# Other orders of reading the moving columns in the series of products behind the last store

## The chip, the core and the metric

The kernel runs on one core of one Trainium2 chip. Its time is the device time of one execution in microseconds (us); the times shown are medians of several executions. A profile is one further execution, recorded instruction by instruction. Its span runs from the first recorded instruction to the last.

## The reference, cut to what matters

The kernel computes one layer of an encoder: two token mixers side by side (windowed attention and a mixture of dilated attentions), merged by gates, then a dense channel mixer, each followed by a layer norm.

```
proj  = h @ w_in
o_a   = windowed_gqa_sink(qa, ka, va, a_sink)
o_b   = dilated_mixture(qb, kb, vb)
gates = sigmoid(h @ w_gate + b_gate)
mixed = g_a * (o_a @ w_br_a) + g_b * (o_b @ w_br_b)
h     = layer_norm(DN_ALPHA * h + mixed @ w_out)
f     = (silu(h @ w_ff_gate) * (h @ w_ff_up)) @ w_ff_down
out   = layer_norm(DN_ALPHA * h + f)
```

There are 512 tokens, 1024 features and 2816 hidden features in the channel mixer. The series of products that the change touches is no part of this: it works on copies of a finished piece of the output, and nothing reads what it leaves in PSUM.

## The kernel before

All work is entered as operations with the engines that may do them, a priority and the tiles that they read and write; a planner in the class Program (lines 100 to 260) places them by estimated costs and emits the instructions in that order. Operations of equal rank keep the order in which they were entered. The tiles are slots of 128 partitions x 512 columns of fp32 (2 KB on each partition, `slot`), wider tiles of 128 x 4 x 512 (`x4`), and eight PSUM banks of 128 x 512 (`bank`).

A product is `mm(out, weights, moving)`: the 128 x 128 weights are loaded into TensorE (LDWEIGHTS, engine PEld in the profile), and then the moving columns, up to 512, are streamed through (MATMUL, engine PE). Most products of the layer read operands of type fp32r, in runs of 256 or 512 columns that follow each other in memory: lines 452 to 454, 1110 to 1112, 1323 to 1325 and 1533 to 1535. Line 932 is one product of the layer that reads its columns, and writes its output, in runs of 32 that do not follow each other.

The last product of the layer is at line 1112, and the last store is issued by SP at line 1569. Behind it lines 1577 to 1616 add a series that the layer doesn't need:

- Lines 1578 to 1586: ACT copies the finished piece xt[3, 1] seven times, into w, x, y (fp32r), u, v (fp32) and b, c (bf16).
- Line 1590: `W(i)` is one of the four 128 x 128 blocks of w; A and B are two PSUM banks.
- `sections` (lines 1594 to 1614) is one operation on PE. Each line of it is a section: 16 products of one kind (8 for fp32, where each product is two instructions), one behind the other, in the order of the text.
- Lines 1595 to 1599 read x in sequence, 512 columns, with varying banks and weights. Lines 1600 to 1604 do the same with 256 columns. Line 1605 uses 64 rows, 1606 and 1607 bf16, 1608 and 1609 fp32. Line 1610 takes its weights with a step of four columns. Line 1611 reads x as two halves in turn: column 0, column 256, column 1, column 257, and so on. Line 1612 has 128 columns, 1613 an output of 64 rows, and 1614 is a series of transposes.

Sections read data that do not change while they run, so no section waits for another engine once the copies are there; the first product waits for the copies into w and x.

Of the kernel before, what the change touches and what calls it, by code (L numbers as in the profile page):

```python
# [15 lines left out]
P = 128  # L16
# [29 lines left out]
PE, ACT, DVE, POOL, SP = "PE", "ACT", "DVE", "POOL", "SP"  # L46
# [53 lines left out]
class Program:  # L100
# [15 lines left out]
    def op(self, alts, fn, reads=(), writes=(), prio=0.0, after=(), abs_prio=None, moves=0.0, extra=0):  # L116
        o = Op()
        o.alts, o.fn = alts, fn
        o.prio = (self.T + prio if abs_prio is None else abs_prio, len(self.ops))
        o.ready, o.done, o.eng = 0.0, None, None  # L120
        deps = set(a for a in after if a is not None)
        for t in reads:
            deps.update(self.writer.get(t, ()))
        for t in writes:
            deps.update(self.writer.get(t, ()))
            deps.update(self.readers.get(t, ()))
        deps.discard(o)
        for t in reads:
            self.readers.setdefault(t, []).append(o)
        for t in writes:  # L130
            self.writer[t] = [o]
            self.readers[t] = []
        o.bufs, o.new = [], []
        o.strict, o.moves, o.extra = self.strict, moves, extra
        o.hold = self.hold and prio <= -150
        for t in list(reads) + list(writes):
            b = self.buf_of(t)
            if b not in o.bufs:
                o.bufs.append(b)
                b.users += 1  # L140
        o.succ = []
        o.left = len(deps)
        for d in deps:
            d.succ.append(o)
        self.ops.append(o)
        return o
# [134 lines left out]
def hybrid_layer(ctx: ExitStack, tc: tile.TileContext, wpack, xT, xtok, sink, bgate,  # L281
                 ln1g, ln1b, ln2g, ln2b, ropec, ropes, maska, maskb, identd, out):
    nc = tc.nc
# [9 lines left out]
    op = pr.op  # L293
    mm = nc.tensor.matmul
    cnt = [0]

    def name(s):
        cnt[0] += 1
        return f"{s}{cnt[0]}"

    def slot(dt=F32, cls=None):
        cls = cls or "gen"
        return Buf("slot", cls, lambda: slab.tile([P, S], dt, tag="slab", bufs=N_SLOT, name=name("sl")))

    def bank(cls):
        return Buf("bank", cls, lambda: psum.tile([P, S], F32, tag="bank", bufs=8, name=name("ps")))

    def x4():
        return Buf("x4", None, lambda: slab.tile([P, 4, S], F32R, tag="x4", bufs=4, name=name("x4")))
# [4 lines left out]
    def fixed(shape, nm):  # L314
        b = Buf("fixed", None, None)
        b.tile = slab.tile(shape, F32, tag=nm, bufs=1, name=nm)
        return b


    def copy(eng, dst, src):  # L320
        if eng == ACT:
            nc.scalar.activation(dst, src, AF.Copy)  # L322
        else:
            nc.vector.tensor_copy(dst, src)
# [61 lines left out]
    ident = fixed([P, P], "ident")  # L386
# [29 lines left out]
    for j in range(KD):  # L416
        st, ap = slot(F32, "xs"), FIRST["x"][j]

        for c0, c1 in ((0, S // 2), (S // 2, S)) if j == 0 else ((0, S),):
            w, sk = c1 - c0, (st, c0)  # L420
# [5 lines left out]
               reads=[sk], writes=[th], abs_prio=ap)  # L426
            op([(DVE, dve(w))], lambda e, j=j, st=st, c0=c0, c1=c1: nc.vector.tensor_tensor(  # L427
                xl[j]()[:, c0:c1], st.t[:, c0:c1], f32(xh[j]()[:, c0:c1]), op=ALU.subtract), reads=[sk, th],
               writes=[tl], abs_prio=ap)
# [8 lines left out]
       reads=[nsink], writes=[nsink], abs_prio=-119)  # L438
# [607 lines left out]
    for f in range(16):  # L1046
        op([(ACT, act(S))], lambda e, f=f: nc.scalar.activation(gz[f].t, gz[f].t, AF.Sigmoid),
           reads=[gz[f]], writes=[gz[f]], after=exps)
# [11 lines left out]
    for f in range(8):  # L1060
        ps = bank("dense")
        wu = unit(U_BRA + f)
        for k in range(KD):
            feat_k(ps, wu, k, MA, lambda k: list(sa[k]))
        mark = op([(DVE, dve(S))], lambda e, f=f, ps=ps: nc.vector.tensor_tensor(gz[f].t, gz[f].t, ps.t, op=ALU.mult),
                  reads=[gz[f], ps], writes=[gz[f]], prio=EV)
# [4 lines left out]
    for f in range(8):  # L1071
# [3 lines left out]
        for k in range(2):  # L1075
            feat_k(ps, wu, k, MB, lambda k: list(sb_[k]), nk=2, col=lambda k, f=f: (k, (f % 4) * P))
        op([(DVE, dve(S))], lambda e, f=f, ps=ps: nc.vector.tensor_tensor(gz[8 + f].t, gz[8 + f].t, ps.t, op=ALU.mult),
           reads=[gz[8 + f], ps], writes=[gz[8 + f]], prio=EV)
        op([(DVE, dve(S))], lambda e, f=f: nc.vector.tensor_tensor(gz[f].t, gz[f].t, gz[8 + f].t, op=ALU.add),
           reads=[gz[f], gz[8 + f]], writes=[gz[f]], prio=EV)  # L1080
# [3 lines left out]
    xt = {(t, j): slot() for t in range(NR) for j in range(2)}  # L1084
# [493 lines left out]
    for n, dt in (("w", F32R), ("x", F32R), ("y", F32R), ("u", F32), ("v", F32)):  # L1578
        scratch[n] = slot(dt)
        op([(ACT, 0.5)], lambda e, n=n: copy(ACT, scratch[n].t, xt[3, 1].t), reads=[(xt[3, 1], 0), (xt[3, 1], 1)],  # L1580
           writes=[scratch[n]])
    scratch["b"], scratch["c"] = [Buf("slot", "gen", lambda: slab.tile([P, 2 * S], BF16, tag="slab", bufs=N_SLOT, name=name("bf")))
                                  for _ in range(2)]
    for n in "bc":
        op([(ACT, 0.5)], lambda e, n=n: copy(ACT, scratch[n].t[:, :S], xt[3, 1].t), reads=[(xt[3, 1], 0), (xt[3, 1], 1)],
           writes=[scratch[n]])
    pa, pb_ = bank("d"), bank("d")
    w, x, y, u, v, bb, cc = [scratch[n] for n in "wxyuvbc"]
    A, B = (lambda: pa.t), (lambda: pb_.t)
    W = lambda i: w.t[:, (i % 4) * P:(i % 4) * P + P]  # L1590
    last = {"skip_group_check": True}
    st = lambda i, m=1: dict(start=(i < m), stop=False, skip_group_check=True)

    def sections(e):
        for i in range(16): mm(A(), W(i), x.t, **st(i))
        for i in range(16): mm(A(), W(0), x.t, **st(i))
        for i in range(16): mm((A, B)[i % 2](), W(i), x.t, **st(i, 2))
        for i in range(16): mm(A(), W(i), (x, y)[i % 2].t, **st(i))
        for i in range(16): mm(A(), W(i), x.t, **st(0))
        for i in range(16): mm(A()[:, :256], W(i), x.t[:, :256], **st(i))  # L1600
        for i in range(16): mm(A()[:, :256], W(0), x.t[:, :256], **st(i))
        for i in range(16): mm((A, B)[i % 2]()[:, :256], W(i), x.t[:, :256], **st(i, 2))
        for i in range(16): mm(A()[:, (i % 2) * 256:(i % 2) * 256 + 256], W(i), x.t[:, (i % 2) * 256:(i % 2) * 256 + 256], **st(i))
        for i in range(16): mm(A()[:, :256], W(i), x.t[:, :256], **st(0))
        for i in range(16): mm(A(), w.t[:64, (i % 4) * P:(i % 4) * P + P], x.t[:64], **st(i))
        for i in range(16): mm(A(), bb.t[:, (i % 4) * P:(i % 4) * P + P], cc.t[:, :512], **st(i))
        for i in range(16): mm(A()[:, :256], bb.t[:, (i % 4) * P:(i % 4) * P + P], cc.t[:, :256], **st(i))
        for i in range(8): mm(A(), u.t[:, (i % 4) * P:(i % 4) * P + P], v.t, **st(i))
        for i in range(8): mm(A()[:, :256], u.t[:, (i % 4) * P:(i % 4) * P + P], v.t[:, :256], **st(i))
        for i in range(16): mm(A(), w.t[:, i % 4:512:4], x.t, **st(i))  # L1610
        for i in range(16): mm(A(), W(i), x.t.rearrange("p (a b) -> p b a", a=2), **st(i))
        for i in range(16): mm(A()[:, :128], W(i), x.t[:, :128], **st(i))
        for i in range(16): mm(A()[:64], w.t[:, (i % 4) * P:(i % 4) * P + 64], x.t, **st(i))
        for i in range(16): nc.tensor.transpose(A()[:, (i % 4) * P:(i % 4) * P + P], u.t[:, (i % 4) * P:(i % 4) * P + P], ident.t)

    op([(PE, 60.0)], sections, reads=[w, x, y, u, v, bb, cc, ident], writes=[pa, pb_])
    pr.run()


# [97 lines left out]
```

## Time and profile before

| what | value |
|---|---|
| median of 2 executions | 849.66 us (849.1 to 850.22) |
| the profiled execution | 849.33 us |
| its span | 847.4 us |
| mean granted TensorE clock over the span | 0.996 |
| start of the series on PE | 782.46 us |
| start of its last section (line 1614) in the chain | 844.74 us |

Times within the trace are counted from the start of the span. In the chain of work that ended last, each row has a start, a length, an engine, an output tile, a line and a count: `3.63 PE ps L1597 x16` is 16 products of line 1597 that held up the end for 3.63 us. In a row for one line, three numbers such as 278/283/283 are the shortest, median and longest duration of one instruction in ns; products overlap, so a duration is longer than the distance from one to the next. In the table by stretch, each row has the bounds, the length, the busy time and count of PE, PEld, DVE, ACT and POOL, then the granted clock, the share of the DMA engines and GB/s.

### The profile page before, as it was taken

The page shows a single profiled execution, that of the slowest core. Times are in us where ns is not written, and L with a number is a line of the kernel's source. Part 1 is how long each engine was busy: PE and PEld are TensorE (multiplying, and loading weights), DVE is VectorE, ACT ScalarE, POOL GpSimd, SP SyncE. Part 2 cuts the span into 40 slices and gives each one's busy share as a digit, 9 for nine tenths or more (in the row PEclk, how much of TensorE's full clock was granted, in tenths as well). Part 3 has the DMA queues.
Part 4 walks back from the last instruction along what each step waited for, and adds up shares of the span by engine and source line. Part 5 has one row for each costly group of instructions (what it writes and reads, how often), then busy time and mean ns, then how long its engine had stood idle before and what let it go on. Part 6 is the DMA issues. An engine that isn't in the chain of part 4 may idle for free.

```text
span 847.4 us, 14091 instructions
## 1 busy us (share of the span) xinstructions
PE 834.2 (98%) x4796; PEld 727.5 (86%) x4797; DVE 670.1 (79%) x1445; ACT 452.7 (53%) x1016; POOL 104.0 (12%) x272
## 2 busy tenths in 40 slices
PE   9999999999999999999999999999999999997999
PEld 6778888888888888787889999999999999985877
DVE  5879988897877976769989979899898988987000
ACT  5555677766646526765345755656556556631000
POOL 0010001000015004101100211112121212100000
PEclk9999999999999999999999999999999999999999
DMA  8552534246171576587616965688777777501000
GB/s 281 179 150 88 162 107 130 100 119 181 51 199 38 149 201 189 167 273 203 164 35 174 237 163 150 160 208 241 204 160 206 217 174 187 144 31 74 1 1 1
DMA packets 71655, 124.94 MB, mean 147 GB/s; under 512 B 8864, under 2 KB 12832, under 8 KB 71584
## 3 DMA queue, kind: packets, MB, share of 16 engines
q1 hardware_dynamic: 61648, 106.08, 39.6%
q0 software_dynamic: 9792, 17.83, 12.8%
q8 instruction: 38, 0.62, 0.3%
q14 instruction: 33, 0.27, 0.1%
q10 hardware_dynamic: 144, 0.13, 0.0%
HBM read 105.40 MB, written 4.46 MB: 130 GB/s over the span
## 4 chain that ended last, share of the span: by engine, by line
PE 87%; DVE 6%; DMA 2%; ACT 2%; issue 1%; SPq 1%; ACTq 0%; DVEq 0%
PE ps L452 9%; PE ps L453 9%; PE ps L454 9%; PE ps L1323 8%; PE ps L1325 8%; PE ps L1324 8%; PE ps L1533 3%; PE ps L1534 3%; PE ps L1535 3%; PE ps L701 2%; PE ps L1110 2%; PE ps L1112 2%; PE ps L1111 2%; ACT sl L322 1%; DMA sl<-wpack 1%
## 5 line engine op out<-in xcount | busy, mean ns | idle before, releaser
L322 ACT ACTIVATE sl<-sl 128x512 fp32r<-128x512 f32 (+3 forms) x402 | 221.2, 585 | 91.0 <-DVE sl L478 32.9
L1213 DVE TENSOR_TENSOR sl<-sl,sl 128x512 fp32r<-128x512 f32 (+3 forms) x294 | 166.6, 609 | 7.2 <-ACT sl L322 6.2
L322 ACT ACTIVATE sl<-ps 128x256 f32<-128x256 f32 (+4 forms) x195 | 83.9, 444 | 115.0 <-PE ps L1325 71.8
L452 PE MATMUL ps<-x,sl 128*128 128x512 f32 (+1 forms) x337 | 134.4, 399 | 0.0
L453 PE MATMUL ps<-x,sl 128*128 128x512 f32 (+1 forms) x337 | 131.8, 391 | 0.2 <-DVE x L427 0.2
L454 PE MATMUL ps<-x,sl 128*128 128x512 f32 (+1 forms) x337 | 131.3, 390 | 0.0
L1323 PE MATMUL ps<-sl,sl 128*128 128x256 f32 x352 | 99.8, 283 | 0.2 <-ACT sl L322 0.2
L1325 PE MATMUL ps<-sl,sl 128*128 128x256 f32 x352 | 99.6, 283 | 0.0
L1324 PE MATMUL ps<-sl,sl 128*128 128x256 f32 x352 | 99.6, 283 | 0.0
L348 DVE TENSOR_TENSOR sl<-sl,sl 128x512 fp32r<-128x512 f32 x130 | 87.3, 685 | 15.5 <-ACT sl L322 10.6
L454 PEld LDWEIGHTS ps<-x,sl 128*128 128x128 f32 x337 | 63.4, 188 | 13.7
L1323 PE MATMUL ps<-x,sl 128*128 128x256 f32 x264 | 74.7, 283 | 0.0
L1325 PE MATMUL ps<-x,sl 128*128 128x256 f32 x264 | 74.7, 283 | 0.0
L1324 PE MATMUL ps<-x,sl 128*128 128x256 f32 x264 | 74.7, 283 | 0.0
L453 PEld LDWEIGHTS ps<-x,sl 128*128 128x128 f32 x337 | 63.6, 189 | 11.1 <-DVE x L427 0.9
L452 PEld LDWEIGHTS ps<-x,sl 128*128 128x128 f32 x337 | 63.5, 189 | 10.9 <-ACT x L322 0.7
L336 POOL DMA_DIRECT2D sl<-wpack x44 | 39.3, 904 | 249.9 <-DMA sl<-wpack 89.1
L1323 PEld LDWEIGHTS ps<-sl,sl 128*128 128x128 f32 x352 | 67.5, 192 | 1.1 <-ACT sl L322 0.6
L1324 PEld LDWEIGHTS ps<-sl,sl 128*128 128x128 f32 x352 | 67.5, 192 | 0.4
L1325 PEld LDWEIGHTS ps<-sl,sl 128*128 128x128 f32 x352 | 67.5, 192 | 0.0
L1324 PEld LDWEIGHTS ps<-x,sl 128*128 128x128 f32 x264 | 50.6, 192 | 0.6
L1323 PEld LDWEIGHTS ps<-x,sl 128*128 128x128 f32 x264 | 50.6, 192 | 0.6
(184 smaller groups left out, 1719.1 us busy)
## 6 DMA issues: line engine op xcount, KB each, us to landing
sl<-wpack SPq DMA_DIRECT2D x243, 256.0 KB, 3.8
sl<-sl SPq DMA_DIRECT2D x108, 128.0 KB, 2.3
wf<-wpack SPq DMA_DIRECT2D x51, 256.0 KB, 5.0
sl<-wpack POOLq DMA_DIRECT2D x44, 256.0 KB, 5.1
wf<-wpack POOLq DMA_DIRECT2D x24, 256.0 KB, 5.3
gz<-sl SPq DMA_DIRECT2D x9, 256.0 KB, 2.3
sl<-gz SPq DMA_DIRECT2D x9, 256.0 KB, 3.7
sl<-xtok SPq DMA_DIRECT2D x8, 256.0 KB, 6.8
```

The costliest lines, as they stand in the source:

```text
L322: nc.scalar.activation(dst, src, AF.Copy)
L336: op([(POOL, 1.0)], lambda e: nc.gpsimd.dma_start(b.t, src2, accum_op=ALU.add), reads=[b], writes=[b], prio=prio, moves=1.65)
L348: op([(DVE, dve(S))], lambda e: nc.vector.tensor_tensor(l.t, src.t, f32(h.t), op=ALU.subtract), reads=[src, h], writes=[l], prio=prio, abs ...
L452: mm(o, a, x0, start=(k == 0 and begins), stop=False, skip_group_check=split)
L453: mm(o, a, x1, start=False, stop=False, skip_group_check=split)
L454: mm(o, b, x0, start=False, stop=(k == nk - 1), skip_group_check=split)
L1213: op([(DVE, dve(w))], lambda e: nc.vector.tensor_tensor(dst(), x(), y(), op=o), reads=reads, writes=writes, prio=prio)
L1323: mm(o, wh, bh[k](), start=(first and k == 0), stop=False, skip_group_check=True)
L1324: mm(o, wh, bl[k](), start=False, stop=False, skip_group_check=True)
L1325: mm(o, wl, bh[k](), start=False, stop=(k == 3), skip_group_check=True)
L1533: mm(ps.t, x0, w[0].t, start=(first and m == 0), stop=False, skip_group_check=True)
L1534: mm(ps.t, x0, w[1].t, start=False, stop=False, skip_group_check=True)
```

## The change

ACT makes two more copies of xt[3, 1], into the first two quarters of a wide tile xw, behind the seven. The body of `sections` is replaced: instead of 20 sections there are 25, nearly all with the type fp32r and the weights `W(i)`, which differ in the order in which the moving columns, and in some the output columns, are walked. `R(t, a)` cuts the first n columns into a pieces and takes one column of each piece in turn. `C(t, a, c)` cuts them into a pieces and takes a run of c columns of each piece in turn.

Counted in the changed file, whose line numbers are these: 1600 is 28 products in sequence; 1601 to 1605 read 2, 4, 16, 128 and 256 pieces in turn; 1606 to 1611 read runs in turn and write their output in the same order; 1612 reads as 1609 does and writes in sequence; 1613 to 1616 have 256 columns (halves in turn, pairs in turn with the output too, every second column, an odd offset of one column); 1617 and 1618 have 384 and 128 columns in halves; 1619 has 18 products over two banks with x and y in turn; 1620 uses 64 rows; 1621 an output of 64 rows; 1622 to 1624 read xw: two runs of 128, two runs of 256, every second column of 1024.

```diff
+    xw = x4()
+    for n in range(2):
+        op([(ACT, 0.5)], lambda e, n=n: copy(ACT, xw.t[:, n], xt[3, 1].t), reads=[(xt[3, 1], 0), (xt[3, 1], 1)], writes=[xw])
     def sections(e):
-        for i in range(16): mm(A(), W(i), x.t, **st(i))
-        for i in range(16): mm(A(), W(0), x.t, **st(i))
...
-        for i in range(16): mm(A(), w.t[:, i % 4:512:4], x.t, **st(i))
-        for i in range(16): mm(A(), W(i), x.t.rearrange("p (a b) -> p b a", a=2), **st(i))
-        for i in range(16): mm(A()[:, :128], W(i), x.t[:, :128], **st(i))
-        for i in range(16): mm(A()[:64], w.t[:, (i % 4) * P:(i % 4) * P + 64], x.t, **st(i))
...
+        R = lambda t, a, n=512: t[:, :n].rearrange("p (a b) -> p b a", a=a)
+        C = lambda t, a, c, n=512: t[:, :n].rearrange("p (a b c) -> p b a c", a=a, c=c)
+        for i in range(28): mm(A(), W(i), x.t, **st(i))
+        for i in range(16): mm(A(), W(i), R(x.t, 2), **st(i))
+        for i in range(16): mm(A(), W(i), R(x.t, 4), **st(i))
+        for i in range(16): mm(A(), W(i), R(x.t, 16), **st(i))
+        for i in range(16): mm(A(), W(i), R(x.t, 128), **st(i))
+        for i in range(16): mm(A(), W(i), R(x.t, 256), **st(i))
+        for i in range(16): mm(C(A(), 8, 32), W(i), C(x.t, 8, 32), **st(i))
+        for i in range(16): mm(C(A(), 16, 8), W(i), C(x.t, 16, 8), **st(i))
+        for i in range(16): mm(C(A(), 2, 4), W(i), C(x.t, 2, 4), **st(i))
+        for i in range(16): mm(C(A(), 2, 2), W(i), C(x.t, 2, 2), **st(i))
+        for i in range(16): mm(C(A(), 128, 2), W(i), C(x.t, 128, 2), **st(i))
+        for i in range(16): mm(C(A(), 16, 2), W(i), C(x.t, 16, 2), **st(i))
+        for i in range(16): mm(A(), W(i), C(x.t, 2, 2), **st(i))
+        for i in range(16): mm(A()[:, :256], W(i), R(x.t, 2, 256), **st(i))
+        for i in range(16): mm(C(A(), 2, 2, 256), W(i), C(x.t, 2, 2, 256), **st(i))
+        for i in range(16): mm(A()[:, :256], W(i), x.t[:, 0:512:2], **st(i))
+        for i in range(16): mm(A()[:, :256], W(i), x.t[:, 1:257], **st(i))
+        for i in range(16): mm(A()[:, :384], W(i), R(x.t, 2, 384), **st(i))
+        for i in range(16): mm(A()[:, :128], W(i), R(x.t, 2, 128), **st(i))
+        for i in range(18): mm((A, B)[i // 3 % 2](), W(i // 3 * 2 + i % 3 // 2), R((x, y)[i % 3 % 2].t, 2), **st(0 if i in (0, 3) else 1))
+        for i in range(16): mm(A(), W(i)[:64], R(x.t[:64], 2), **st(i))
+        for i in range(16): mm(A()[:64], W(i)[:, :64], R(x.t, 2), **st(i))
+        for i in range(16): mm(A()[:, :256], W(i), xw.t[:, 0:2, 0:128], **st(i))
+        for i in range(16): mm(A(), W(i), xw.t[:, 0:2, 0:256], **st(i))
+        for i in range(16): mm(A(), W(i), xw.t[:, 0:2].rearrange("p a c -> p (a c)")[:, 0:1024:2], **st(i))
```

More of the change, by code (lines that the diff above doesn't have):

```diff
@@ L1594, in sections @@
     def sections(e):
[L1595 to L1612, printed above, removed]
-        for i in range(16): mm(A()[:64], w.t[:, (i % 4) * P:(i % 4) * P + 64], x.t, **st(i))
@@ L1614, in sections @@
-        for i in range(16): nc.tensor.transpose(A()[:, (i % 4) * P:(i % 4) * P + P], u.t[:, (i % 4) * P:(i % 4) * P + P], ident.t)
-    op([(PE, 60.0)], sections, reads=[w, x, y, u, v, bb, cc, ident], writes=[pa, pb_])
+        R = lambda t, a, n=512: t[:, :n].rearrange("p (a b) -> p b a", a=a)
+        C = lambda t, a, c, n=512: t[:, :n].rearrange("p (a b c) -> p b a c", a=a, c=c)
+        for i in range(28): mm(A(), W(i), x.t, **st(i))
+        for i in range(16): mm(A(), W(i), R(x.t, 2), **st(i))
@@ L1617, in hybrid_layer @@
+        for i in range(16): mm(A(), W(i), xw.t[:, 0:2, 0:256], **st(i))
+        for i in range(16): mm(A(), W(i), xw.t[:, 0:2].rearrange("p a c -> p (a c)")[:, 0:1024:2], **st(i))
+    op([(PE, 60.0)], sections, reads=[w, x, y, u, v, bb, cc, xw, ident], writes=[pa, pb_])
     pr.run()
```

## The prediction

> **What bounds the kernel now.** I read the page's shares first, then the chain of work that ended last from the last store on, then single lines of the series and the granted clock by stretch.
>
> ```profile
> span 847.4 us, 14091 instructions
> PE 834.2 (98%) x4796; PEld 727.5 (86%) x4797; DVE 670.1 (79%) x1445; ACT 452.7 (53%) x1016; POOL 104.0 (12%) x272
> ```
>
> PE is busy for 98% of the span, and the edit touches only PE's last stage and two copies on ACT. In that stage the chain is nothing but PE, section behind section (columns: start, length, engine, output, line, count):
>
> ```profile
> 781.26 0.63 ACT sl L322
> 781.89 0.53 ACTq L1712
> 782.42 0.04 issue
> 782.46 6.01 PE ps L1595 x16
> 788.47 3.65 PE ps L1596 x16
> 792.12 3.63 PE ps L1597 x16
> ...
> 806.83 1.92 PE ps L1602 x16
> ...
> 812.59 3.85 PE ps L1605 x16
> ...
> 820.00 1.75 PE ps L1607 x16
> ...
> 832.07 3.79 PE ps L1610 x16
> 835.86 3.45 PE ps L1611 x16
> 839.31 1.74 PE ps L1612 x16
> ...
> 844.74 1.75 PE ps L1614 x16
> ```
>
> The reader is to see three things. First, everything from 782.46 to 844.74 + 1.75 = 846.49 us, 64.03 us in all, is products one behind the other: whatever they cost is on the path, with no cover. Second, a product of 512 columns read in sequence takes 3.63 / 16 = 0.227 us (L1597), but L1611, which already reads its moving columns from two halves in turn, takes 3.45 / 16 = 0.2157 us: that order costs nothing and saves 11 ns. Third, the saving is per product, not per column: 256 columns in sequence take 1.92 / 16 = 0.120 us, and the bf16 section of 256 columns (L1607) 0.1093 us, again 11 ns apart. I take 0.2157 and 0.1093 us for an order that costs nothing, and 0.227 and 0.120 for a sequence.
>
> The first section is long because of the clock:
>
> ```profile
> 782.00:787.00 5.00, 4.54 (x11) 3.57 (x12) 0.00 (x0) 3.00 (x6) 0.00 (x0) 0.50 0.15 52
> 788.30:800.00 11.70, 11.70 (x53) 9.68 (x52) 0.00 (x0) 0.00 (x0) 0.00 (x0) 1.00 0.01 1
> ```
>
> The granted clock (third number from the end) is 0.50 in the first 5 us and 1.00 after. It stays so, since the stage begins in the same way.
>
> **The change part by part.** Line numbers with "new" are those of the changed kernel. Nothing ahead of the last store moves: on DVE, POOL and SP the instruction order is the same, on ACT two copies come behind the seven that are there, and PE's rows differ from the series on.
>
> Two copies into xw. ACT's last two scratch copies stand in this row:
>
> ```profile
> 783.87 1.13 ACT L322 ACTIVATE bf<-sl 128x512 bf16<-128x512 f32 x2
> ```
>
> They end at 785.00; two more of the same length end near 786.1 us. PE waits for xw only at new L1622, over 50 us later by the sum below, so the copies are hidden by the sections ahead; with that cover gone they would cost 1.13 us. The first product waits for w and x, still ACT's first two copies, so the start stays at 782.46. PE waits for y at new L1619, for a copy that ends long before.
>
> The old series goes: 64.03 us. The new series is 25 sections with 414 products:
> - New L1600, 28 in sequence: the first 16 as L1595, 6.01 us; 12 more at 0.227: 2.72. Sum 8.73.
> - 274 products of 512 columns: fourteen sections of 16 that read in some other order, the 18 of new L1619, and new L1606 and L1623 (taken as sequences below). At 0.2157: 59.10 us.
> - Of these, new L1606 alternates whole runs of 32 columns and new L1623 reads two runs of 256. The nearest row for runs is L932, whose source and output both go in runs of 32, beside L1600 in sequence:
>
> ```profile
> L932 PE MATMUL ps<-sl,sl x32: 278/282/366, 270.9 to 360.1; 128*128 128x256 f32 x32
> L1600 PE MATMUL ps<-sl,sl x16: 278/283/283, 802.8 to 804.6; 128*128 128x256 f32 x16
> ```
>
> The medians are 282 and 283 ns: long runs neither gain nor lose, so these two sections go at 0.227: 32 x 11 ns = 0.36 us more.
> - Five sections of 256 columns: new L1613, L1614, L1615 as L1607, 1.75 each; new L1616 (odd offset) and L1622 (two runs) as L1602, 1.92 each. Sum 9.09.
> - 384 columns (new L1617): halfway between 0.1093 and 0.2157, an estimate, 0.1625 x 16 = 2.60. 128 columns (new L1618): as L1612, 1.74, where the weight load already sets the pace.
> - 64 rows (new L1620): L1605 took 0.22 us more than L1597 at the change of shape; add 0.22.
>
> Sum 8.73 + 59.10 + 0.36 + 9.09 + 2.60 + 1.74 + 0.22 = 81.84 us if no order costs anything; against 64.03 that is +17.81 us.
>
> What is not in the trace is the price of the coarse orders. Two rows bound it. The free one is L1611. The dear one is L1610, where the weights, not the moving columns, are read with a step of four columns, 16 bytes:
>
> ```profile
> L1610 PEld LDWEIGHTS ps<-sl,sl x16: 308/316/328, 831.7 to 835.2; 128*128 128x128 f32 x16
> L1611 PEld LDWEIGHTS ps<-sl,sl x16: 187/189/190, 835.5 to 838.7; 128*128 128x128 f32 x16
> ```
>
> 128 columns at a step cost 316 - 189 = 127 ns more than in sequence, 1.0 ns per column. So a reader on TensorE's side does pay for a step. Lower end per column 0 (L1611), upper end 1.0 ns extra; harsher still, the whole pace of L1610, which its load sets: 3.79 / 16 = 0.237 us for 128 columns of weights, 1.85 ns per column.
>
> Section by section: new L1601, L1612, L1613, L1617 to L1621 read two pieces in turn, and new L1608, L1609, L1614 two pieces in runs of four or two: nearest L1611, free. New L1602 (four pieces) is also nearer to two pieces than to 128: free. New L1605, L1610, L1615, L1624 step by 8 bytes or take pairs: two neighbours per visit, between the rows; I take free and keep 1.85 ns per visit as the upper end. New L1611 takes pairs from 16 pieces: the same. New L1604 (128 pieces, a step of exactly L1610's 16 bytes) pays: 16 x 512 x 1.0 ns = 8.2 us. New L1603 (16 pieces, a step of 128 bytes) comes back to a place only after 16 columns, which is nearer to never than to every second: it pays 8.2 too.
>
> Total +17.81 + 16.4 = +34.2 us. Against the profiled execution's own 849.33 us (span 847.4) that gives 883.5 us. The median shown, 849.66, is 0.33 above it, which is noise here.
>
> [...]
>
> **The rivals.**
> - No order costs anything. For it: L1611, and L932. Then the sum is 81.84 and the time 849.33 + 17.8 = 867.1 us. If the two sections in runs, the odd offset and the two runs of 256 also drop their 11 ns (64 x 11 ns = 0.7), it is 866.4. This is the case that ends on the other side: 2% above the median is 849.66 x 1.02 = 866.65, so this one mechanism, every order at L1611's pace, can land on either side of that bound (2% is about what a measurement of this kernel can tell from no change). It lands within 2% as long as all the orders together add less than 0.2 us to 866.4. Against it: L1610's load.
> - Every visit to another place costs the load's 1.85 ns, and only two places are kept open. Then new L1602, L1603 and L1604 take 512 x 1.85 = 0.947 us per product, 11.7 us more each, 35.1; the sections of pairs (new L1605, L1610, L1611, L1624) take 256 visits, 0.474 us, 4.1 more each, 16.5; new L1615 2.0. 867.1 + 53.6 = 920.7 us. For it: L1610's pace, and that a sequence, one visit per four columns, would be just at 0.237 us, near its 0.227. Against it: nothing in the trace reads moving columns so.
> - Four pieces pay with 16 and 128, at 1.0 ns, and pairs are free: 867.1 + 3 x 8.2 = 891.7 us. [...]
> - The outputs pay, not the inputs. New L1607 to L1611 and L1614 write PSUM in runs of 8, 4 or 2 columns; the nearest row, L932 with runs of 32, shows no price. Were each to double, 5 x 3.45 + 1.75 = 19.0 us: 886.1 us. [...]
>
> **How the numbers follow.** Chances: the forecast (16 and 128 pieces pay) 0.34; no order pays 0.18, of which half lies within 2%; every visit pays 0.22; four pieces pay too 0.12; outputs pay 0.08; mixtures above 921 us 0.05; faster than by the sum of free orders 0.01. The time is the likeliest case's, 883.5, whose own range is 875 to 892 (price 0.5 to 1.5 ns per column). The range for 8 in 10 is 866.3 to 920: from the free orders to nearly every visit paid. Slower by over 2%: 0.90; within 2%: 0.09; faster: 0.01, since the path only gains products and the cheapest pace known, 0.2157, still gives 866.4.
>
> **What would show it.** In the changed kernel's chain, L1600 near 8.7 us, L1601 at 3.45, and 3.45 for all sections of 512 columns but L1603 and L1604 at about 11.7, L1606 and L1623 at 3.63. A long L1602 says that four pieces pay; long L1605, L1610, L1615 and L1624 that visits are paid; long L1608 and L1609, with L1612 short (the same reading as L1609, output in sequence), that the output pays. All at 3.45 to 3.63 says that no order pays. Wrong on other grounds: a start other than 782.46, or a clock that stays at 0.50 beyond L1600.

## The result, and the profile after

The changed kernel takes 898.34 us (897.88 to 898.79) against 849.66 us before: 1.0573 times as long, with a 95% interval of 1.0527 to 1.0618. The forecast was 883.5 us, in a range of 866.3 to 920. The profiled execution took 897.88 us, its span 896.0.

The layer did not move: the series starts at 782.30 us, 0.16 us earlier than before. The whole difference lies in the series. This is the chain of work that ended last in the changed kernel, from the series on, with the sections that the argument needs (start, length, engine, output, line, count):

```profile
782.30 8.25 PE ps L1600 x28
790.55 3.45 PE ps L1601 x16
794.00 4.52 PE ps L1602 x16
798.52 6.96 PE ps L1603 x16
805.48 7.38 PE ps L1604 x16
812.86 7.22 PE ps L1605 x16
820.08 3.78 PE ps L1606 x16
823.86 3.70 PE ps L1607 x16
827.56 4.00 PE ps L1608 x16
831.57 5.43 PE ps L1609 x16
837.00 7.31 PE ps L1610 x16
844.31 7.05 PE ps L1611 x16
851.36 5.33 PE ps L1612 x16
856.68 1.78 PE ps L1613 x16
858.47 2.68 PE ps L1614 x16
861.15 3.62 PE ps L1615 x16
864.77 1.96 PE ps L1616 x16
...
884.17 3.65 PE ps L1623 x16
887.83 7.25 PE ps L1624 x16
```

Three groups can be read off the lengths. Two pieces in turn (L1601) cost 3.45 us, as L1611 of the kernel before did. Orders with long runs (L1606, L1607, L1623) cost 3.65 to 3.78. The other orders of 512 columns shown cost more: four pieces and runs of four or two from halves 4.00 to 5.43 us, and the rest meet a ceiling. 16, 128 or 256 pieces, pairs from 16 or 128 pieces, and every second column all lie between 6.96 and 7.38 us, about twice a sequence's 3.63 (L1597 of the kernel before), whatever the step. In the prediction a step of 16 bytes was to cost 3.45 + 8.2 us and a step of 8 bytes nothing. They cost nearly the same, 7.38 (L1604) and 7.22 (L1605).

### The profile page after: what moved, and what is told of

The parts are those of the page before. It is cut to its first block, busy times and chain, and to the rows that moved or that the text cites. A ratio compares the mean times of both kernels' runs of the same rounds, so it can differ in the third digit from the quotient of the medians.

```text
span 896.0 us, 14282 instructions
## 1 busy us (share of the span) xinstructions
PE 883.0 (99%) x4891; PEld 751.4 (84%) x4891; DVE 669.9 (75%) x1445; ACT 453.7 (51%) x1018; POOL 103.2 (12%) x272
## 4 chain that ended last, share of the span: by engine, by line
PE 89%; DVE 6%; ACT 2%; DMA 1%; issue 1%; SPq 1%; ACTq 0%; DVEq 0%
PE ps L452 9%; PE ps L453 9%; PE ps L454 9%; PE ps L1323 8%; PE ps L1325 8%; PE ps L1324 8%; PE ps L1533 3%; PE ps L1534 3%; PE ps L1535 3%; PE ps L701 2%; PE ps L1110 2%; PE ps L1112 2%; PE ps L1111 2%; PE ps L602 1%; PE ps L601 1%
```

## The experiments

In the first six kernels below the layer is as before, and only the sections of the series are others; the last two have no series. "Pieces" and "places" are where the columns come from; "in turn" is one column, or one run, from each. The kernels under "two places", "more places", "types", "two streams" and "outputs" were executed once each and are read section by section in that trace; 16 fp32r products with all 128 rows that read 512 columns in halves took 3.45 us in every trace that has them, but for outputs of 64 rows (3.60) and weights with a step of four columns (3.79).

**Halves in place of the dear orders.** The twelve sections whose price was in doubt (4, 16, 128, 256 pieces, runs of 2 and 4, every second column) read two halves in turn and write in sequence.

```diff
-        for i in range(16): mm(A(), W(i), R(x.t, 4), **st(i))
+        for i in range(16): mm(A(), W(i), R(x.t, 2), **st(i))
...
-        for i in range(16): mm(C(A(), 128, 2), W(i), C(x.t, 128, 2), **st(i))
+        for i in range(16): mm(A(), W(i), R(x.t, 2), **st(i))
...
-        for i in range(16): mm(A()[:, :256], W(i), x.t[:, 0:512:2], **st(i))
+        for i in range(16): mm(A()[:, :256], W(i), R(x.t, 2, 256), **st(i))
```

> The changed kernel with the twelve dear sections (4, 16, 128 and 256 pieces, runs of 2 and 4, every second column) reading two halves in turn instead, with outputs in sequence. If the orders alone carry the price, ten sections of 512 columns drop from 62.45 us together to 34.5 and two of 256 columns from 6.30 to 3.6: 898.3 - 30.7 = 867.6 us, the sum of the prediction without any price (867.1). If something else in the longer series costs time (its number of products, the wide tile), it stays above 875.

Measured: 867.77 us (866.82 to 869.29), 1.0222 times the kernel before (1.0205 to 1.024), and so 30.6 us below the changed kernel where 30.7 were expected. The orders carry the price; the longer series and the wide tile cost nothing beside their products. It is also what the prediction's case without any price (867.1 us) would have looked like.

**Two places at many distances, and runs.** Three theories were on the table: the price follows the distance between successive columns; it follows the number of places; or columns are read two at a time out of lines of 16 bytes. `G(t, a, k)` takes one column in turn from each of a places that lie k columns apart.

```diff
+        G = lambda t, a, k, n=512: t[:, :n].rearrange("p (g a k) -> p g k a", a=a, k=k)
+        for i in range(16): mm(A(), W(i), G(x.t, 2, 2), **st(i))
+        for i in range(16): mm(A(), W(i), G(x.t, 2, 4), **st(i))
...
+        for i in range(16): mm(A(), W(i), xw.t[:, 0:2, 0:256].rearrange("p a c -> p c a"), **st(i))
...
+        for i in range(16): mm(A(), W(i), C(x.t, 4, 2), **st(i))
...
+        for i in range(16): mm(A(), W(i), C(x.t, 64, 4), **st(i))
```

> The series holds other sections; the layer ahead of it is untouched. Sections read two places in turn at distances of 8, 16, 32, 64, 128, 256, 512, 1024 and 2048 bytes, three of them with 256 columns too, and then runs of columns in turn. Theory of lines and pairs: TensorE takes columns two at a time and holds the 16-byte lines of the last pair, so two places cost 0.216 to 0.227 us per product of 512 columns at every distance; runs of four columns from any number of places cost about 0.23 to 0.25 (each line is used up in one visit), pairs from any number of places 0.34 to 0.45. Theory of distance: the price follows the distance in bytes between successive columns, so two places at 16 bytes cost 0.46 as one column of each 16 bytes did, at 128 bytes 0.43, at 512 bytes 0.28, and only 1024 and 2048 bytes are free. Theory of the number of places: two places free everywhere, as in the first, but four pieces in runs of four cost more than two (0.28 against 0.25) and 16 pieces in runs of four 0.43.

The chain of this kernel: L1602 has the two places 8 bytes apart, L1603 16 bytes, L1610 2048 bytes; L1617 is pairs from four pieces, L1618 to L1620 runs of four from 4, 16 and 64 pieces, L1621 pairs from eight pieces.

```profile
792.07 3.63 PE ps L1602 x16
795.69 3.45 PE ps L1603 x16
...
819.87 3.45 PE ps L1610 x16
...
838.27 7.18 PE ps L1617 x16
845.45 4.28 PE ps L1618 x16
849.73 3.95 PE ps L1619 x16
853.68 3.70 PE ps L1620 x16
857.38 7.96 PE ps L1621 x16
```

Two places cost 3.45 us at each of the eight distances from 16 to 2048 bytes, so the theory of distance falls. Runs of four, 16 bytes and so a line used up per visit by the third theory, cost less the more pieces there are: 4.28 us from 4, 3.95 from 16, 3.70 from 64. The theory of number is near for four pieces (0.268 us per product against 0.28) and far off for 16 (0.247 against 0.43), so the number of places alone does not decide either. Lines and pairs, which allowed 0.23 to 0.25 for all of them, misses the four pieces, and pairs from eight pieces (0.498) lie above its 0.34 to 0.45. The one exception among two places is informative: neighbours in the order 0, 2, 1, 3 (L1602) cost exactly a sequence's 3.63.

**More places.** The wide tile is filled in all four quarters here, by two more copies on ACT.

```diff
+        for i in range(16): mm(A(), W(i), G(x.t, 4, 4), **st(i))
...
+        for i in range(16): mm(A(), W(i), xw.t[:, 0:4, 0:128].rearrange("p a c -> p c a"), **st(i))
...
+        for i in range(16): mm(A(), W(i), G(x.t, 8, 4), **st(i))
...
+        for i in range(16): mm(A(), W(i), G(x.t, 16, 4), **st(i))
```

> The series holds other sections, and the wide tile is filled in all four quarters; the layer ahead is untouched. Four places in turn at 16, 64, 128, 256, 512 and 2048 bytes, six places at 256 bytes, eight at 16, 64 and 256 bytes, sixteen at 16 and 128 bytes, and runs of two and four from places 2048 bytes apart. Theory of the number of places: four places cost 0.28 us per product at every distance, eight near 0.36, sixteen 0.43. Theory of distance: four places at 16 bytes cost 0.46, at 128 bytes 0.43, at 512 bytes 0.28, at 2048 bytes 0.216, whatever the number. Theory of lines and pairs, with the lines of the last pair alone held: four and more places cost 0.43 to 0.46 at every distance, and the 0.28 of four pieces at 512 bytes is left unexplained; pairs from two places 2048 bytes apart cost 0.34 as at 1024 bytes.

Four places at 16 bytes (L1602) and at 2048 bytes (L1607), eight at 16 bytes (L1610), sixteen at 16 bytes (L1613):

```profile
791.76 4.29 PE ps L1602 x16
...
813.78 4.53 PE ps L1607 x16
...
825.32 7.68 PE ps L1610 x16
...
847.88 7.36 PE ps L1613 x16
```

Four places cost 4.29 to 4.53 at every distance, which the theory of number expected and the theory of distance did not. But eight cost 7.04 to 7.84 and sixteen 6.93 to 7.36, where it expected eight to lie between four and sixteen: with eight the ceiling is reached. Six do lie between: over 384 columns six places took 3.73 us and four 3.27. Lines and pairs, which held only the lines of the last pair, expected 0.43 to 0.46 us from four places on, so it falls in that form too.

**Types, and small weights.** Here bb and cc are the copies in bf16, u and v those in fp32.

```diff
+        for i in range(16): mm(A(), bb.t[:, (i % 4) * P:(i % 4) * P + P], R(cc.t, 2), **st(i))
...
+        for i in range(16): mm(A(), bb.t[:, (i % 4) * P:(i % 4) * P + P], R(cc.t, 256), **st(i))
...
+        for i in range(8): mm(A(), u.t[:, (i % 4) * P:(i % 4) * P + P], R(v.t, 128), **st(i))
+        for i in range(8): mm(A(), u.t[:, (i % 4) * P:(i % 4) * P + P], R(v.t, 256), **st(i))
...
+        for i in range(16): mm(A()[:32], W(i)[:, :32], x.t, **st(i))
+        for i in range(16): mm(A()[:32], W(i)[:, :32], R(x.t, 2), **st(i))
```

> The series holds other sections; the layer ahead is untouched. bf16 products whose moving columns step by 2, 4, 8 and 32 columns or come from two and four pieces, fp32 products (two passes each) in the same orders, and fp32r products with 32 weight columns. If lines of 16 bytes set the price (lines and pairs), bf16 is priced by bytes: every second column (4 bytes) 0.22 to 0.23 us, every fourth (8 bytes) 0.45, every eighth (16 bytes) 0.46; fp32 at 0.429 us per pass has time for a line per pair and stays within 0.43 to 0.47 in every order. If the order of columns as such is priced, every second bf16 column costs 0.45 and the fp32 passes double to about 0.9. The 11 ns of a sequence: if they come from the weight load of the next product reading beside the columns, 32 weight columns bring the sequence of 512 from 0.227 to about 0.219, and 128 columns in sequence to 0.056; if they belong to the start of a sequence, 0.227 stays and 128 columns cost 0.065 against 0.054 in halves.

In the chain, L1603 is bf16 from two pieces, L1606 to L1608 bf16 with steps of 16, 8 and 4 bytes, L1612 and L1613 fp32 with steps of 16 and 8 bytes, L1615 and L1616 a sequence and two halves with 32 weight columns:

```profile
794.48 7.75 PE ps L1603 x16
...
829.76 14.40 PE ps L1606 x16
844.16 7.23 PE ps L1607 x16
851.39 3.62 PE ps L1608 x16
...
884.48 14.40 PE ps L1612 x16
898.88 7.20 PE ps L1613 x16
...
909.76 3.71 PE ps L1615 x16
913.47 3.45 PE ps L1616 x16
```

bf16 is priced by bytes. A line of 16 bytes per column costs 14.40 / (16 x 512) = 1.76 ns, two columns per line 7.23 / (16 x 256) = 1.77 ns per line, four per line 3.62 / (16 x 128) = 1.77 ns per line: one price, 1.77 ns per line opened. Steps longer than 16 bytes cost no more: 16 pieces, a step of 64 bytes, took 13.71 us (L1605). fp32 is the same, 1.76 ns per line in each of its two passes.

The granted clock has to be read beside this. The page of this kernel gives it in 40 slices of 23.5 us:

```profile
PEclk9999999999999999999999999999999998659999
```

It is 0.6 in the slice from 798.1 to 821.6 us, 0.5 in the one from 821.6 to 845.1, and 0.9 or more in every slice behind them, with PE busy all the time in the chain. The mean over the span is 0.973, where the changed kernel has 0.996; if the clock was 0.50 while it was low, that is (0.996 - 0.973) x 939 / 0.5 = 43 us, an estimate. So bf16 from 16 and 64 pieces (L1605, L1606) lies where the clock was near half, with most of L1604 and perhaps part of L1607, and L1608 and the fp32 sections lie in slices of 0.9 or more. There fp32 pays the same 0.90 us per pass as bf16 near the half clock, and L1608 the same 1.77 ns per line: the price of a line did not follow the clock here. A bf16 product with a step of 16 bytes at the full clock was not run.

I had expected a ceiling of 0.46 us per product for bf16 and about that per pass for fp32; it is 0.90 in both. And two pieces in turn, free in fp32r, cost bf16 0.484 us. So fp32r is the exception: a line per column costs it 0.461 us, half of 0.90.

From this came the theory of **two streams**. In fp32r one stream takes the first, third, fifth column in the order read and the other the rest, and each opens a 16-byte line in 1.77 ns. A sequence of 512 columns is then 128 lines for each stream: 128 x 1.77 = 0.227 us, what it costs. Halves in turn give each stream a sequence of its own, 64 lines, 0.113 us, so another bound is left, 0.216, which no order of 512 fp32r columns went below; I take it for the array's own time, which no run shows by itself. The kernel above bears out two bounds: with 32 weight columns a sequence grows from 0.96 / 16 us at 128 columns to 3.71 / 16 at 512, 1.79 ns for each of the 96 lines more, and halves from 0.89 / 16 to 3.45 / 16, 0.417 ns per column. Every second column is 256 visits per stream and 256 lines, 0.453. A line per column is also 256 per stream, 0.453, where 16, 128 and 256 pieces took 0.435, 0.461 and 0.451. By this theory that is the ceiling.

In this form the theory is not complete. Four places put two places into each stream and should cost 0.453 us too, where 0.268 to 0.283 was measured, pairs of columns from halves should cost 0.453 and took 0.333 to 0.339, runs of four should cost 0.227 and took 0.231 to 0.268, and pairs from eight pieces go above the ceiling (0.498). And a reader that takes the columns in pairs and opens the lines of both at once counts the same lines in every order run here; nothing below tells it from two streams.

**Two streams, tested.** The theory had to forecast orders, most of which had not been seen.

```diff
+        for i in range(16): mm(A(), W(i), x.t.rearrange("p (a b s) -> p s b a", a=2, s=2), **st(i))
+        for i in range(16): mm(A(), W(i), x.t.rearrange("p (a b s) -> p s b a", a=2, s=4), **st(i))
...
+        for i in range(16): mm(A(), w.t[:, i % 2:256:2], x.t, **st(i))
+        for i in range(16): mm(A(), w.t[:, i % 2:256:2], R(x.t, 2), **st(i))
+        for i in range(16): mm(A(), w.t[:, i % 4:512:4], R(x.t, 2), **st(i))
...
+        for i in range(16): mm(A(), bb.t[:, (i % 4) * P:(i % 4) * P + P], G(cc.t, 2, 4), **st(i))
+        for i in range(16): mm(A(), bb.t[:, (i % 4) * P:(i % 4) * P + P], G(cc.t, 2, 8), **st(i))
```

> The series holds other sections; the layer ahead is untouched. Theory of two streams, formed after the first four runs: fp32r columns are read by two streams, one taking the first, third, fifth column in the order read, the other the rest, and each stream opens a 16-byte line in 1.77 ns, or serves a column from the line it has open. It expects: every second column of two halves in turn 0.227 us per product of 512 (128 lines per stream), where every second column in one piece cost 0.452; every fourth column of two halves in turn 0.453; neighbours of one line in the order 0, 2, 1, 3 0.227, as a sequence; weights with a step of two columns no dearer than in sequence (64 lines), so 0.216 beside halves and 0.227 beside a sequence; weights with a step of four 0.235 also beside halves, set by the load. bf16 has one stream: two places in turn cost about 0.48 at every distance beyond a line, and two places 8 bytes apart, in one line, 0.216. The rival, that the order as such is priced by places and runs: every second column of two halves 0.45 as in one piece, the steps of weights all alike dearer, and the bf16 place 8 bytes apart at 0.48.

L1602 and L1603 are every second and every fourth column of two halves, L1605 every second column in one piece; L1606 is a sequence whose weights have a step of two columns; L1607 and L1608 are halves whose weights have steps of two and four; L1613 and L1614 are bf16 from two places in one line and in two:

```profile
792.16 3.63 PE ps L1602 x16
795.78 7.25 PE ps L1603 x16
...
806.68 7.25 PE ps L1605 x16
813.93 3.73 PE ps L1606 x16
817.66 3.45 PE ps L1607 x16
821.11 3.79 PE ps L1608 x16
...
834.15 3.47 PE ps L1613 x16
837.62 7.76 PE ps L1614 x16
```

All but L1606 came out as two streams had it: 3.63, 7.25, 7.25, 3.45, 3.79, 3.47 and 7.76 us for 16 products. L1606 took 3.73 us, 0.233 us per product, where the 0.227 of a sequence was expected, and 256 columns in halves beside such weights 0.119 for 0.112. The 0.48 for bf16 from two lines (L1614) was the earlier measurement repeated, at other distances; a stream that opens a line per visit would give 0.90. The rival expected 0.45 us per product for L1602, the step of L1605; it took half of that.

**Outputs.** To close the prediction's rival that the outputs pay, they were put in runs while the reading stayed in sequence or in halves, and the runs were read alone.

```diff
+        for i in range(16): mm(C(A(), 2, 2), W(i), x.t, **st(i))
...
+        for i in range(16): mm(C(A(), 128, 2), W(i), x.t, **st(i))
...
+        for i in range(16): mm(C(A(), 2, 2), W(i), R(x.t, 2), **st(i))
...
+        for i in range(16): mm(A(), W(i), C(x.t, 128, 2), **st(i))
```

> The series holds other sections; the layer ahead is untouched. Outputs in runs of 2, 8 and 32 columns with the moving columns in sequence or in halves, the same orders on the moving side alone with the output in sequence, and bf16 columns in runs of 2, 4 and 8 from two places. If only the reading is priced, the first six sections cost 0.227 us per product and the next two 0.216, as with an output in sequence, and the runs read alone cost what they cost with the output in the same order: 0.25 (runs of 4), 0.45, 0.44, 0.23 and 0.236. If the output pays, as the rival of the prediction had it, runs of two columns on the output alone cost 0.34 to 0.45. bf16, by one stream that opens a line in 1.77 ns: runs of 8 columns use up a line per visit, 64 lines, 0.216; runs of 4 between 128 and 64 lines, at most 0.25; runs of 2 between those and 256 lines, 0.23 to 0.45.

```profile
790.46 3.63 PE ps L1602 x16
...
801.34 3.63 PE ps L1605 x16
...
812.22 3.45 PE ps L1608 x16
...
823.14 7.22 PE ps L1611 x16
```

Outputs in pairs cost nothing (L1602, L1605 beside a sequence, L1608 beside halves), and pairs read alone from 128 pieces cost 7.22, about what they cost with the output turned as well (7.31). Pairs from 16 pieces read alone cost 7.46, more than the 7.05 with the output turned; that difference is unexplained, but it goes against a price of the output. The rival is closed. bf16 in runs of 8, 4 and 2 from two places took 0.216, 0.226 and 0.272 us.

**The layer in halves.** If a sequence of fp32r columns is bound by its lines, so are the layer's own products. Two kernels without the series test this: the layer alone, and the layer with 3138 products read in halves. Token order within a tile is free as long as the products agree; it is set right where tokens become weights, by a step of two. The weights of the two products by token are laid out by the host.

```diff
+    def halves(ap):
+        return ap.rearrange("p (a b) -> p b a", a=2)
...
-                mm(o, wh, bh[k](), start=(first and k == 0), stop=False, skip_group_check=True)
+                mm(o, wh, halves(bh[k]()), start=(first and k == 0), stop=False, skip_group_check=True)
...
-                a0, a1 = us[0].t[:, t * P:(t + 1) * P], us[1].t[:, t * P:(t + 1) * P]
+                c = (t // 2) * 256 + t % 2 if fine else (t % 2) * 256 + t // 2
+                a0, a1 = us[0].t[:, c:c - c % 256 + 256:2], us[1].t[:, c:c - c % 256 + 256:2]
...
-    units += [w_ff_down[128 * k:128 * k + 128] for k in range(22)]
+    units += [turned(w_ff_down[128 * k:128 * k + 128]) for k in range(22)]
```

> Leaves out the whole series of products behind the last store and its copies, so that only the layer is left, whose output it gives. By the trace of before, the last store was issued at 781.36 us and PE's series ran from 782.46 to 846.49: the time should fall by 60 to 64 us, to about 786 to 789 us, if the stores' landing is all that is left behind.

> The layer alone, with 3138 of its products reading the moving columns from two halves in turn: 624 of 512 columns in the gates and branch products and 1848 of 256 columns in the channel mixer, whose token order is so turned and set right by weights read with a step of two columns, and 666 of 512 columns in the two products by token, whose weights the host lays out with even columns ahead of odd ones. If halves in turn cost 0.216 and 0.112 us in the layer as in the series, and PE bounds it throughout, 1290 x 11 ns and 1848 x 8 ns are saved: 14.2 + 14.8 = 29 us below the layer alone, near 758 us. Rival: other engines or the loads with a step of two take up part of it, so that less than 15 us are saved, or the stepped loads cost 0.235 as those with a step of four did and the 666 products by token get no faster.

Measured: the layer alone 786.48 us, within the 786 to 789 expected, 0.9259 times the kernel before (0.9246 to 0.9271); in halves 762.42 us, 0.8974 (0.8961 to 0.8986). The halves are worth 24.1 us where 29 were expected. First the page's shares and a product of the channel mixer in the layer alone, then the same in halves:

```profile
PE 771.1 (98%) x4477; PEld 677.4 (86%) x4477; DVE 670.3 (85%) x1445; ACT 448.9 (57%) x1009; POOL 103.3 (13%) x272
L1325 PE MATMUL ps<-sl,sl x352: 278/283/288, 459.1 to 743.4; 128*128 128x256 f32 x176
PE 86%; DVE 6%; DMA 3%; ACT 2%; issue 1%; SPq 1%; DVEq 0%; ACTq 0%
```

```profile
PE 743.1 (98%) x4477; PEld 668.3 (88%) x4477; DVE 666.5 (88%) x1445; ACT 446.7 (59%) x1009; POOL 103.9 (14%) x272
L1331 PE MATMUL ps<-sl,sl x352: 275/275/275, 450.5 to 720.3; 128*128 128x256 f32 x176
PE 77%; DVE 13%; DMA 3%; issue 2%; ACT 2%; SPq 1%; DVEq 0%; ACTq 0%
```

PE's busy time falls by 28.0 us, nearly the 29 expected, and the median product by 8 ns. The span falls by 24.0 (784.7 to 760.7), so PE's idle time grew by 4.0 us, from 13.6 to 17.6. Of PE's waits, those on ACT grew from 0.7 to 2.4 us and those on DVE from 4.3 to 5.9; in the chain DVE's share rises from 6 to 13%. So the 5 us that are missing went to waits on ACT and DVE for the most part; no run shortened these waits to test it.

## Why the prediction was right, and where its steps were not

- **Direction, place and the sum without prices were right.** All of the difference is in the series, with no cover. The sum without any price was 81.84 us for the series and 867.1 us for the time; with halves in the dear places, 867.77 was measured.
- **The step that failed is the section by section pricing: "two neighbours per visit, between the rows; I take free", and 1.0 ns per column for 16 and 128 pieces.** The likeliest case had two dear sections at 3.45 + 8.2 us each. They were 6.96 and 7.38, together 9.0 us less than taken. In their place ten sections taken as free cost 23.3 us more than taken: 1.07 (L1602), 3.77 (L1605), 0.55 (L1608), 1.98 (L1609), 3.86 (L1610), 3.60 (L1611), 1.88 (L1612), 0.93 (L1614), 1.87 (L1615), 3.80 (L1624). 23.3 - 9.0 and 0.2 of small things make the 14.5 us by which the series, 895.08 - 782.30 = 112.78 us, exceeds the 98.24 forecast. New L1607, which the list of sections leaves out and the sum takes at 0.2157 us per product, is one of the small things, 0.25 us. So the change cost 48.7 us where 34.2 were forecast, and that the total came this near was partly luck: two errors of opposite sign.
- **The row was the right one, read too loosely.** L1610's load was a reader that opens a line per column; its 1.85 ns per column lies near the 1.77 ns per line of the moving columns. I took the excess over a sequence (1.0 ns) as a price per column, instead of asking how many lines each order opens. The rival "every visit pays" did ask, with 1.85 ns, and gave the sections of pairs and of every second column (0.474 against 0.441 to 0.457 us measured) nearly right; it was wrong where it had one reader and not two, by the theory above, which doubled 16 and 128 pieces to 0.947, and it put four pieces there too, which cost 0.283.
- **The other rivals.** That no order pays fell at once (L1604). That four pieces pay with 16 and 128 was right in kind, but four pieces cost 1.07 us per section and not 8.2. That the outputs pay (886.1 us) was wrong: outputs in runs cost nothing. That every visit pays came to 920.7 us, too much by its dear pieces.
- **The clue was in the trace.** A sequence at 0.227 and halves at 0.2157: I called the 11 ns a saving per product, because a bf16 section of 256 columns also lay 11 ns below. By the theory of two streams it is the difference between a product bound by its lines and one that is not. With 32 weight columns the sequence and the halves took 60 and 56 ns at 128 columns, 118 and 109 at 256, 232 and 216 at 512: the gap grows with the columns. Neither thing that I had expected of these sections, 0.219 us for the sequence of 512 or a gap that stays at 11 ns, came out.
- **Halves of 256 columns** took 0.111 to 0.112 us and not bf16's 0.1093; with 32 weight columns they took 0.109, so the 2 to 3 ns appear beside a weight load of 128 columns.
- **The start and the clock** were as forecast but for 0.5 us in the first section (8.25 for 8.73). That section took 8.03 to 9.41 us over the kernels with the series of 28, with the clock still low for part of it (in the changed kernel 0.50 from 782 to 785 us, 0.62 over the next and 1.00 from 786 on).
- **The unit of 16 bytes, pairs and outputs.** The prediction counts two columns at a step of 8 bytes, and in its second rival four of a sequence, as one visit; no row of before shows that unit. The runs do: 16 bf16 products cost 14.40, 7.23 and 3.62 us at steps of 16, 8 and 4 bytes, and no more than the first at 64 (13.71). That pairs and every second column are free, as the forecast and the rival of 891.7 us had it, no run shows: every second fp32r column took 0.453 us per product and pairs from 128 pieces 0.457, against 0.216 for halves. Nor does any run show the doubling by which the rival of 886.1 us priced the outputs: with the moving columns in sequence, outputs in runs of two cost 0.227 us, as a sequence does.

What stays open: two places in one stream. Four pieces in fp32r (two for each stream) cost 0.268 to 0.283 us, runs of two from halves 0.333 to 0.339, and two pieces in bf16 0.484, all between a line per visit and a line held open for each place. How a stream keeps part of a second line was not settled, nor why eight places and pairs from eight or 16 pieces spread from 0.440 to 0.498 us around the ceiling of 0.453. The two streams themselves are inferred from times; no view shows them.

## What to carry to other kernels

Count the lines of 16 bytes that an order opens, per reader, and multiply by the price of one line as the trace shows it (1.77 ns here); a product costs the larger of that and the bound that no order went below (0.216 us for 512 fp32r columns here). The count held here for sequences, steps and two places in fp32r and for sequences and steps in bf16 and fp32; for orders that come back to a line soon it gave too much (four places, or pairs from two, in fp32r; two places in bf16), so measure those. For fp32r count the odd and the even columns in the order read apart: two halves in turn are then cheaper than a sequence, by 5% of a product of 512 columns, and an order of tokens or weights that permits them can be free (the layer took 24.1 us less with them). Where two rows for the same work differ by a few nanoseconds, ask which bound each of them shows before calling the difference an overhead.

## What the runs showed of the hardware that was not expected

- A sequence is not the fastest order in fp32r: 0.227 us for 512 columns against 0.216 from two places in turn, at any distance from 16 to 2048 bytes.
- bf16 and fp32 have no such gain and pay more for steps: 0.90 us (fp32: per pass) for 512 columns 16 bytes apart, against 0.461 in fp32r. A line opened cost 1.76 to 1.77 ns both where the page has a granted clock of 0.6 and 0.5 and where it has 0.9 or more.
- The granted clock was 0.6 and 0.5 in two slices of 23.5 us within dear bf16 sections, with PE busy all the time in the chain; the fp32 sections, just as long (13.97 and 14.40 us), lie in slices of 0.9 or more.
- Weights with a step of two columns cost nothing beside 512 columns read in halves (0.216), and a little beside a sequence (0.233 for 0.227) or 256 columns in halves (0.119 for 0.112); with a step of four they set 0.237.
- An output in runs of two columns costs a product nothing (0.227 and 0.216).
